# Shifted taps of a causal convolution: added by accumulating transfers on GpSimd's queue in place of VectorE additions

## The chip, the cores and the metric

The kernel runs on one core of a Trainium2 chip. The metric is the device time of one execution in microseconds (us). Five engines have instruction streams of their own and run them in order: TensorE (PE in the profile; PEld is its weight load), VectorE (DVE), ScalarE (ACT), GpSimd (POOL) and SyncE (SP). Transfers are issued by an engine's queue (here SP's and POOL's, a few by ACT) and carried out by 16 DMA engines. Tiles lie in SBUF, 128 partitions wide; products land in PSUM banks.

## The reference: what is computed

One decoder layer on 256 tokens of width 2048, in float32: a combined input projection, two token mixers, an output projection, a gated MLP with a causal depthwise convolution, and a last gate. The change touches the MLP alone:

```python
h = rms_norm(x, ffn_norm_g[i])
u = h @ w_up[i]                                   # 2048 x 11264
a, g = jnp.split(u, 2, axis=-1)                   # 5632 channels each
a = causal_dwconv(a, conv_w[i], conv_b[i])        # width 3, along the tokens
x = x + (jax.nn.gelu(a, approximate=False) * g) @ w_down[i]
```

Per channel the convolution at token s is `w2*a[s] + w1*a[s-1] + w0*a[s-2] + b`, with zeros ahead of the first token.

## The kernel before, in words

**Products.** Each float32 operand is split in two parts, hi (a rounded copy, a CAST on ACT, L1224) and lo (the difference, a subtraction on DVE, L1226), and each product is made of three matmuls: hi x hi, hi x lo, lo x hi (L356, L357, L358 in the MLP). So each block of weights goes through four stations: a load by SP's queue (L1201), the cast on ACT, the subtraction on DVE, the matmuls on PE. Blocks are called units; a plain unit ("p") is one 128-row slice of the weights with 12 matmuls of 512 columns, and some pairs of slices are computed by a seven-product scheme in four short units of 3 to 6 matmuls ("a", "b").

**Groups.** w_up is worked through in 11 groups of 512 + 512 columns (`up_group`, strings in ORDERS give the order of the units of each group: 18 units where the group has one seven-product pair, 20 where it has two). What a group leaves in PSUM goes to EZ (`up_rows`, L1082, and `summed`, L1089), is turned so that channels lie on partitions (`turned`: a 32x32 transpose on DVE, L194, from EZ to Y, and then 16 transfers of 64 KB from Y back to EZ, seen as Z, L200: six from POOL's queue, ten from SP's), and then convolved (`up_act`). All this is done during the units of the next group, between the casts and subtractions of its weights.

**The convolution of one group** has ten jobs: four `scaled(j)` on ACT (each one L1108, which writes w2*a + b to the tile c_, a part of xs, and two L1111, which write w1*a and w0*a to the two taps in Y); `shifted(1)` and `shifted(2)`, which add the taps to c_, one and two tokens later (L1115); `gelu` (ACT, L1118, in place on c_); `gated` (DVE, L1121, times the gate half); `parts_of` (the split in hi and lo for w_down, L150 and L151); and `left` (sums for the seven-product scheme, L456 to L460, one transfer of 512 KB to DRAM, L1068).

**What sets the order.** Each job is hung behind a unit of the next group: ACT_AT holds, for the ten jobs, the number of the unit in the next group. A scheduler in the build lays the instructions out on each engine and may put a job somewhat before or behind that place; the engines then run their lists in order. Parts have a limited number of tiles (eight, four units' worth, while w_up is worked on), so a cast that comes too early waits until PE has released a tile. The last group's jobs don't use ACT_AT: they hang behind fixed units of the work with w_down.

## Time and profile before

| what | value |
|---|---|
| time, median of 3 runs (range) | 1232.63 us (1232.27 to 1233.55) |
| span of the profiled execution, first to last instruction | 1230.1 us |
| PE busy | 1224.3 us (100%) |
| DVE busy | 982.2 us (80%) |
| ACT busy | 749.1 us (61%) |
| POOL busy | 186.8 us (15%) |
| DMA engines, mean busy share over 440 to 930 us | 0.75 |

The profiled execution is told by its span, 1230.1 us from first to last instruction; the median of the runs is 2.5 us above it. The MLP's first half, where the convolutions are, runs from about 440 to 930 us of the span. In the tables below, times of a timeline are from the span's start; "idle before" is how long the engine stood still before an instruction, with what ended that wait; "to landing" is the time from the issue of a transfer to the semaphore that tells of its end. Groups are counted from 1 here: the second group's convolution lies at about 535 to 555 us, the fifth's at 665 to 683, the sixth's at 705 to 724.

### The profile page before, as it was taken

How to read it: one execution, taken by the hardware profiler on the slowest of the kernel's cores; microseconds unless marked ns; L12 is line 12 of the kernel's file. 1: busy time of each engine (PE TensorE's matmuls, PEld its weight loads, DVE VectorE, ACT ScalarE, POOL GpSimd, SP SyncE). 2: the span in 40 equal slices, each digit the busy share in tenths (PEclk: the TensorE clock that was granted, in tenths of full speed). 3: DMA queues.
4: the chain of work that ended last, by engine and by line, in shares of the span. 5: the costliest groups of instructions: out<-in, count | busy, mean ns of one | idle time of the engine just before them, and what ended most of it. 6: DMA issues, size and time to landing. Idle time of an engine off the chain costs nothing.

```text
span 1230.1 us, 16375 instructions
## 1 busy us (share of the span) xinstructions
PE 1224.3 (100%) x5593; PEld 1031.5 (84%) x5593; DVE 982.2 (80%) x1216; ACT 749.1 (61%) x1097; POOL 186.8 (15%) x347
## 2 busy tenths in 40 slices
PE   9999999999999999999999999999999999999998
PEld 7999988888888888888888888888888888888887
DVE  6788857665565689789998898898788999999773
ACT  7567545565554555766676676757657655556652
POOL 2011237243304301011101101110110000050000
PEclk9999999999999999999999999999999999999999
DMA  9566587686557786777687678756797895886670
GB/s 306 182 195 196 171 231 225 186 221 186 163 181 221 221 312 207 242 220 234 210 273 240 182 259 264 226 177 222 228 316 243 296 374 203 266 251 211 200 225 35
DMA packets 131444, 276.89 MB, mean 225 GB/s; under 512 B 14921, under 2 KB 24641, under 8 KB 131233
## 3 DMA queue, kind: packets, MB, share of 16 engines
q1 hardware_dynamic: 119456, 257.40, 66.0%
q0 software_dynamic: 11520, 18.29, 5.3%
q8 instruction: 44, 0.72, 0.2%
q14 instruction: 39, 0.32, 0.1%
q10 hardware_dynamic: 385, 0.16, 0.0%
HBM read 247.99 MB, written 8.93 MB: 209 GB/s over the span
## 4 chain that ended last, share of the span: by engine, by line
PE 99%; DMA 0%; SPq 0%; DVE 0%; ACT 0%; issue 0%; DVEq 0%
PE up L357 12%; PE up L358 11%; PE up L356 11%; PE tg L345 9%; PE tg L346 9%; PE tg L347 9%; PE pg L356 3%; PE pg L357 3%; PE pg L358 3%; PE dnP L1276 1%; PE dnP L1274 1%; PE dnP L1275 1%; PE upP L356 1%; PE upP L358 1%; PE upP L357 1%; PE gt L357 1%
## 5 line engine op out<-in xcount | busy, mean ns | idle before, releaser
L291 DVE TENSOR_TENSOR lo<-raw,hi 128x1024 fp32r<-128x1024 f32 (+3 forms) x130 | 153.3, 1181 | 107.8 <-ACT hi L289 107.4
L358 PE MATMUL up<-part,x2T 128*128 128x512 f32 x608 | 236.6, 389 | 0.0
L357 PE MATMUL up<-part,x2T 128*128 128x512 f32 x608 | 236.5, 389 | 0.0
L1224 ACT CAST part<-raw 128x1024 fp32r<-128x1024 f32 (+1 forms) x144 | 145.5, 1021 | 114.6 <-PE up L358 35.0
L289 ACT CAST hi<-raw 128x1024 fp32r<-128x1024 f32 (+3 forms) x130 | 132.3, 1017 | 123.7 <-PE tg L347 63.4
L1226 DVE TENSOR_TENSOR part<-raw,part 128x1024 fp32r<-128x1024 f32 (+1 forms) x140 | 164.4, 1182 | 26.7 <-ACT part L1224 20.8
L356 PE MATMUL up<-part,x2T 128*128 128x512 f32 x608 | 185.0, 389 | 0.0
L356 PEld LDWEIGHTS up<-part,x2T 128*128 128x128 f32 x608 | 114.2, 188 | 23.6
L358 PEld LDWEIGHTS up<-part,x2T 128*128 128x128 f32 x608 | 114.2, 188 | 23.6
L357 PEld LDWEIGHTS up<-part,x2T 128*128 128x128 f32 x608 | 114.1, 188 | 23.6
L347 PE MATMUL tg<-hi,hT 128*128 128x512 f32 x288 | 113.6, 395 | 0.0
L346 PE MATMUL tg<-lo,hT 128*128 128x512 f32 x288 | 113.2, 393 | 0.0
L345 PE MATMUL tg<-hi,hT 128*128 128x512 f32 x288 | 112.5, 397 | 0.0
L200 POOL DMA_DIRECT2D EZ<-Y x66 | 35.0, 538 | 372.8 <-issue 205.2
L1224 ACT CAST part<-u36r 128x1024 fp32r<-128x1024 f32 (+1 forms) x46 | 47.8, 1041 | 34.6 <-PE up L358 16.3
L1226 DVE TENSOR_TENSOR part<-u36r,part 128x1024 fp32r<-128x1024 f32 (+1 forms) x46 | 55.6, 1209 | 11.0 <-ACT part L1224 6.7
L347 PEld LDWEIGHTS tg<-hi,hT 128*128 128x128 f32 x288 | 54.1, 188 | 11.1
L346 PEld LDWEIGHTS tg<-lo,hT 128*128 128x128 f32 x288 | 54.1, 188 | 10.9
L345 PEld LDWEIGHTS tg<-hi,hT 128*128 128x128 f32 x288 | 53.8, 188 | 10.7
L1226 DVE TENSOR_TENSOR part<-u32r,part 128x1024 fp32r<-128x1024 f32 (+1 forms) x44 | 50.4, 1148 | 11.9 <-ACT part L1224 9.2
L1224 ACT CAST part<-u32r 128x1024 fp32r<-128x1024 f32 (+1 forms) x44 | 43.3, 990 | 21.3 <-PE up L358 9.0
L357 PE MATMUL pg<-lo,hT 128*128 128x430 f32 (+1 forms) x156 | 55.7, 357 | 0.0
(889 smaller groups left out, 2722.0 us busy)
## 6 DMA issues: line engine op xcount, KB each, us to landing
raw<-in_w_up_dram SPq DMA_DIRECT2D x78, 512.0 KB, 5.1
raw<-in_w_in_dram SPq DMA_DIRECT2D x71, 512.0 KB, 4.3
u36r<-in_w_up_dram SPq DMA_DIRECT2D x43, 512.0 KB, 5.0
raw<-in_w_down_dram SPq DMA_DIRECT2D x41, 512.0 KB, 6.2
u32r<-in_w_up_dram SPq DMA_DIRECT2D x34, 512.0 KB, 5.1
raw<-in_w_out_dram SPq DMA_DIRECT2D x32, 512.0 KB, 4.8
xs<-in_w_up_dram SPq DMA_DIRECT2D x21, 512.0 KB, 5.1
w2b<-in_w_down_dram SPq DMA_DIRECT2D x20, 512.0 KB, 5.5
```

Source lines behind the costliest of these rows:

```text
L200: (other if other and (4 * a + b) % 3 else pool).dma_start(out=c[32 * b : 32 * b + 32, a::4], in_=y[32 * a : 32 * a + 32, :, b])
L289: act.copy(hi, raw)
L291: dve.tensor_sub(lo, raw, f32(hi))
L345: pe.matmul(o, ah, hi[:, i, :], start=first, stop=False)
L346: pe.matmul(o, ah, lo[:, i, :], start=False, stop=False)
L347: pe.matmul(o, al, hi[:, i, :], start=False, stop=last)
L356: pe.matmul(o, ah, hi, start=start, stop=False)
L357: pe.matmul(o, ah, lo, start=False, stop=False)
L358: pe.matmul(o, al, hi, start=False, stop=stop)
L1224: act.copy(r32(hi), raw)
L1226: dve.tensor_sub(r32(lo), raw, hi)
L1274: pe.matmul(o, ah, hi, start=first, stop=False)
```

## The change

The two additions L1115 leave DVE. Each becomes one transfer from the tap in Y to c_ with the operation "add", issued by POOL's queue: it reads the tap, adds it to what c_ holds, and writes c_. Both write the same tile, so the second waits for the landing of the first, and `gelu` waits for both. In the same step ACT_AT puts the four scalings behind units 6 to 9 of the next group (9 to 12 before) and the two additions behind units 9 and 11 (13 and 14 before); `gelu`, `gated`, `parts_of` and `left` keep 15 to 18.

```diff
-ACT_AT = (9, 10, 11, 12, 13, 14, 15, 16, 17, 18)
+ACT_AT = (6, 7, 8, 9, 9, 11, 15, 16, 17, 18)
...
             def shifted(d):
-                return lambda: dve.tensor_add(c_[:, :, d:S], taps[d - 1][:, :, 0 : S - d], c_[:, :, d:S])
+                return lambda: pool.dma_start(out=c_[:, :, d:S], in_=taps[d - 1][:, :, 0 : S - d], accum_op=ALU.add)
```

**On ACT, second group.** The list of ACT around this group's last scaling and its gelu (`part_0_...` is the hi part of a unit, named by its number; L1693 empties a PSUM bank). Before:

```order
L1108 ACTIVATE xs<-EZ,cT 128x256
L1111 ACTIVATE Y<-EZ,cT 128x256 x2
L1693 COPY xs<-upP_4878 128x512
L1224 CAST part_0_5041<-u36r 128x1024
L1224 CAST part_0_5062<-u32r 128x1024
L1224 CAST part_0_5093<-u36r 128x1024
L1118 ACTIVATE xs<-xs 128x1024
L1224 CAST part_0_5073<-raw_0_4919 128x1024
```

With the change:

```order
L1108 ACTIVATE xs<-EZ,cT 128x256
L1111 ACTIVATE Y<-EZ,cT 128x256 x2
L1224 CAST part_0_5002<-raw_0_4876 128x1024
L1224 CAST part_0_5030<-raw_0_4904 128x1024
L1224 CAST part_0_5012<-xs 128x1024
L1693 COPY xs<-upP_4878 128x512
L1224 CAST part_0_5062<-u32r 128x1024
L1224 CAST part_0_5042<-u36r 128x1024
L1118 ACTIVATE xs<-xs 128x1024
L1224 CAST part_0_5093<-u36r 128x1024
L1224 CAST part_0_5073<-raw_0_4919 128x1024
```

The last scaling has moved ahead of three casts, the gelu ahead of one; it now waits for the landing of both transfers, and the cast of part 5093 stands behind it.

**On ACT, second group, its first scalings.** Before:

```order
L1224 CAST part_0_4933<-u36r 128x1024
L1224 CAST part_0_4976<-u36r 128x1024
L1108 ACTIVATE xs<-EZ,cT 128x256
L1111 ACTIVATE Y<-EZ,cT 128x256 x2
L1224 CAST part_0_4961<-u32r 128x1024
L1108 ACTIVATE xs<-EZ,cT 128x256
L1111 ACTIVATE Y<-EZ,cT 128x256 x2
L1224 CAST part_0_4946<-xs 128x512
```

With the change:

```order
L1224 CAST part_0_4936<-u36r 128x1024
L1108 ACTIVATE xs<-EZ,cT 128x256
L1111 ACTIVATE Y<-EZ,cT 128x256 x2
L1108 ACTIVATE xs<-EZ,cT 128x256
L1111 ACTIVATE Y<-EZ,cT 128x256 x2
L1224 CAST part_0_4986<-u36r 128x1024
L1224 CAST part_0_4970<-u32r 128x1024
L1108 ACTIVATE xs<-EZ,cT 128x256
L1111 ACTIVATE Y<-EZ,cT 128x256 x2
L1224 CAST part_0_4952<-xs 128x512
```

Parts 4976, 4961 and 4946 are 4986, 4970 and 4952 here. Two scalings now stand ahead of the cast that was first, and a third ahead of the cast of 512 columns from xs.

**On POOL, second group.** Before, the six transfers of one group are followed by those of the next:

```order
L200 DMA EZ<-Y 32x2x256 [waits DMASW1_49]
L200 DMA EZ<-Y 32x2x256 [waits DMASW2_49]
L200 DMA EZ<-Y 32x2x256 [waits DMASW3_49,DVE_49,Activation_49]
L200 DMA EZ<-Y 32x2x256 [waits DMASW4_49]
L200 DMA EZ<-Y 32x2x256 [waits DMASW5_49]
```

With the change the two additions stand between them:

```order
L200 DMA EZ<-Y 32x2x256 [waits DMASW1_49]
L200 DMA EZ<-Y 32x2x256 [waits DMASW2_49]
L1115 DMA xs<-Y 128x4x255 [waits DMASW4_49,Activation_49]
L1115 DMA xs<-Y 128x4x254 [waits DMASW3_49,Activation_49]
L200 DMA EZ<-Y 32x2x256 [waits DMASW5_49,DVE_49,Activation_49]
L200 DMA EZ<-Y 32x2x256 [waits DMASW6_49]
```

The first addition waits for ACT's scalings, the second for the landing of the first, and behind them the next group's transfers stand in the queue.

## The prediction

> **What bounds the kernel now.** I read the page first, then PE's waits, then the table of busy times over the stretch in which the convolutions run.

> ```profile
> span 1230.1 us, 16375 instructions
> PE 1224.3 (100%) x5593; PEld 1031.5 (84%) x5593; DVE 982.2 (80%) x1216; ACT 749.1 (61%) x1097; POOL 186.8 (15%) x347
> PE 99%; DMA 0%; SPq 0%; DVE 0%; ACT 0%; issue 0%; DVEq 0%
> PE warm L100 <- DVE ones L96: 1.1, 1, 1.1
> ...
> 440.00:930.00 490.00, 490.00 (x2163) 405.87 (x2162) 426.40 (x448) 321.56 (x428) 40.10 (x75) 1.00 0.75 237
> ```

> The columns of the last row are the stretch, its sum, and the busy time of PE, PEld, DVE, ACT and POOL, then PE's granted clock, the DMA share and GB/s. PE is busy for all of the 490 us, at full clock, one matmul behind the other; its longest wait anywhere is the 1.1 us at the start, and 99% of the chain that ended last is PE. DVE is busy for 426 of those 490 us, ACT for 322. So nothing that DVE gives up can shorten this stretch: 1230.1 - 1224.3 = 5.8 us is all the idle time PE has, and it lies outside it. The change can only cost time, and costs some where a unit's hi or lo part comes later than PE is ready for it.

> **What is removed, and what hides it.**

> ```profile
> L1115 DVE TENSOR_TENSOR xs<-Y,xs x22: 1209/1213/1217, 506.4 to 946.6; 128x1020 f32<-128x1020 f32 x11, 128x1016 f32<-128x1016 f32 x11
> ```

> 22 x 1.213 = 26.7 us of DVE, all beside busy PE: worth 0.

> **What one accumulating transfer costs (L, from issue to landing).** No such transfer is in the trace. The nearest rows:

> ```profile
> q0 software_dynamic: 11520, 18.29, 5.3%
> ...
> sums<-Sp POOLq DMA_DIRECT2D x9, 512.0 KB, 3.9
> ...
> EZ<-Y POOLq DMA_DIRECT2D x66, 64.0 KB, 2.5
> ...
> EZ<-Y SPq DMA_DIRECT2D x110, 64.0 KB, 2.6
> ...
> DMA to landing us min/median/max: 2.9/3.9/5.2
> ...
> DMA to landing us min/median/max: 3.8/5.1/9.6
> ```

> (The last two are the ranges of the sums' 512 KB to DRAM and of the 512 KB loads on SP's queue in this stretch.) POOL's queue moved 18.29 MB in 5.3% of 1230.1 us, 3.56 us per MB. One addition is 128 x 1020 x 4 B = 0.522 MB, so as a plain copy 1.86 us; what is left of the two POOL rows, 3.9 - 1.9 = 2.0 and 2.5 - 0.2 = 2.3, is the fixed part, about 2.2. An accumulation reads two streams where a copy reads one. If that costs nothing, L = 2.2 + 1.9 = 4.1 (low end 2.9, the fastest row of sums); if the engines' time doubles, 2.2 + 3.7 = 5.9; if it triples (read, read, write, in pieces of 1020 B), 7.8. Weight loads share the engines, and between the fastest and the median load lie 1.3 us of queueing; so 9.1 at the high end. I take doubling with half of that queueing: **L = 6.5** (an estimate). The second addition waits for the first, and the gelu for the second; with about 0.1 us for each of three hand-overs the chain from the end of the last scaling to the gelu is 2L + 0.3 = 13.3 us, where DVE needed two passes of 1.2 us.

> [...]

> **The room in the second group.** Its rows on ACT, SP and PE:

> ```profile
> 526.11 6.52 SPq L200 DMA_DIRECT2D EZ<-Y  x10
> ...
> 535.25 0.60 ACT L1108 ACTIVATE xs<-EZ,cT 128x256 f32<-128x256 f32 x1
> 535.75 0.90 ACT L1111 ACTIVATE Y<-EZ,cT 128x256 f32<-128x256 f32 x2
> 536.55 1.03 ACT L1224 CAST part<-u32r 128x1024 fp32r<-128x1024 f32 x1
> 537.49 0.60 ACT L1108 ACTIVATE xs<-EZ,cT 128x256 f32<-128x256 f32 x1
> ...
> 538.79 0.61 ACT L1224 CAST part<-xs 128x512 fp32r<-128x512 f32 x1
> 539.30 1.06 ACT L1224 CAST part<-raw 128x1024 fp32r<-128x1024 f32 x1
> ...
> 544.86 0.89 ACT L1111 ACTIVATE Y<-EZ,cT 128x256 f32<-128x256 f32 x2
> ...
> 550.21 1.05 ACT L1224 CAST part<-u36r 128x1024 fp32r<-128x1024 f32 x1 [2.08 <-issue]
> 551.17 1.05 ACT L1118 ACTIVATE xs<-xs 128x1024 f32<-128x1024 f32 x1
> ...
> 720.21 1.05 ACT L1224 CAST part<-u36r 128x1024 fp32r<-128x1024 f32 x1 [2.07 <-issue]
> 721.17 1.05 ACT L1118 ACTIVATE xs<-xs 128x1024 f32<-128x1024 f32 x1
> ...
> 540.22 0.39 PE L356 MATMUL upP<-part,x2T 128*128 128x512 f32 x1
> ...
> 552.91 0.62 PE L356 MATMUL up<-part,x2T 128*128 128x512 f32 x2
> ```

> One scaling takes 1.30 us of ACT (535.25 to 536.55), a cast 0.94 (536.55 to 537.49), the half cast 0.51. SP issues the last of its ten transfers at about 532.0, and these land after a median of 2.6 (EZ<-Y on SPq, above); so the first scaling cannot start before 534.6, however early it stands in the list. From there by the new order: two scalings to 537.2, two casts to 539.1, the third scaling to 540.4, the half cast to 540.9, the fourth scaling to 542.2; before, it ended at 545.7.
> - The half cast starts at 540.4 instead of 538.8, 1.6 later. Counted through the order, PE's first product with its tile is the row at 540.22, 0.8 behind that cast's end of 539.4. So **PE loses 0.8** whatever L is.
> - The cast of part 5093 (550.21) now stands behind the gelu. The first product on it is the second of the two at 552.91, at 553.14; so the cast must start by 552.1 and the gelu by 551.1. The room is 551.1 - 542.2 = 8.9, with PE 0.8 late 9.7. **13.3 - 9.7 = 3.6** lost.

> Behind the waiting gelu in ACT's list stand all casts of the coming units, and behind each cast DVE's subtraction and PE. The sixth group has the same order (its gelu at 721.17 stands behind the same cast with the same 2 us gap); I take it alike: 2 x 4.4 = 8.8 us.

> **The other groups.** The fifth stands for the six (first, third, fifth, seventh, ninth and tenth) whose jobs run beside longer units:

> ```profile
> 662.63 1.05 ACT L1224 CAST part<-u36r 128x1024 fp32r<-128x1024 f32 x1
> ...
> 673.12 0.90 ACT L1111 ACTIVATE Y<-EZ,cT 128x256 f32<-128x256 f32 x2
> ...
> 680.27 1.05 ACT L1224 CAST part<-raw 128x1024 fp32r<-128x1024 f32 x1 [1.66 <-PE up L358]
> 681.23 1.05 ACT L1118 ACTIVATE xs<-xs 128x1024 f32<-128x1024 f32 x1
> ...
> 619.87 0.60 ACT L1108 ACTIVATE xs<-EZ,cT 128x256 f32<-128x256 f32 x1
> ...
> 628.02 0.56 ACT L1693 COPY xs<-upP 128x512 f32<-128x512 f32 x1
> ...
> 634.31 1.05 ACT L1118 ACTIVATE xs<-xs 128x1024 f32<-128x1024 f32 x1
> ```

> Its first scaling moves to 662.6; four scalings and two casts end at 669.8 instead of 673.9. Room 681.2 - 669.8 = 11.4, so the gelu is 13.3 - 11.4 = 1.9 late. But here ACT had waited for PE to release a tile (680.27): the casts are three units of 12 matmuls ahead, 3 x 12 x 0.227 = 8.2 us, less 2.3 for the cast and the subtraction: 5.9 of cover, of which I count on 4, since ACT has the next group's PSUM to empty right behind. Lost: 0. (0.227 is the distance of two matmuls, 540.22 and the next; 2163 in 490 us.) In the fourth and eighth the new list has all four scalings in a row: from 619.9 to 625.1, instead of to 628.0; room 634.3 - 625.1 = 9.2; 4.1 late, the cover is somewhere between 0 and 5.9, I take 3: 1.1 each, 2.2 together. The last group's jobs keep their far places: 0.

> **POOL, SP and the DMA engines.**

> ```profile
> 482.35 3.19 POOL L200 DMA_DIRECT2D EZ<-Y  x6 [48.94 <-ACT part L1224]
> 526.66 3.16 POOL L200 DMA_DIRECT2D EZ<-Y  x6 [41.12 <-issue]
> ...
>   ACT part L1224: 12.7, 8
> ```

> On POOL only the next group's six transfers stand behind the additions, due a group of some 44 us after their own predecessors and so over 20 us after the additions: 0, and with that cover gone the scalings behind them would come late in turn. SP is not moved past anything. 22 additions at 3.7 us of all 16 engines add 82 us to a share of 0.75 over 490 us, which makes 0.92; ACT waits for the stretch's weight loads for 12.7 us in 8 waits today (last row), all covered, and I add 1 us for later loads.

> Sum: 8.8 + 2.2 + 1 = **12 us slower**; 1230.1 + 12 in the span, 1232.6 + 12 = **1245 us** by the median.

> **Rivals.**
> - *Copy price.* Where an addition costs no more than a copy, L = 4.1 and the chain 8.5, within every room. What is left is the early scalings, 2 x 0.8 = 1.6: 1234 us, no change that can be measured. For it: POOL's 512 KB row of 3.9. Against it: the second stream read, the pieces of 1020 B, and that the room of 9.7 is used up at L = 4.7.
> - *Triple price*, slower yet. L = 7.8 to 9.1, chain 15.9 to 18.5: second and sixth 2 x 6.2 to 2 x 8.8, fourth and eighth 2 x 3.7 to 2 x 6.3, the six others 0.5 to 3.1 each, with the 1.6 in all 24 to 50 us: 1257 to 1283.
> [...]
> - *Faster.* Only where freed DVE makes a late lo part earlier; but PE waits for none in 490 us. 1229 at best.

> ```profile
> L200 POOL DMA_DIRECT2D EZ<-Y x66: 533/536/567, 482.3 to 915.2; - x66
> ```

> **How the numbers follow.** The forecast (L from 4.9 to 7.6; 1235 to 1255) 0.45; copy price 0.25; triple price 0.22; descriptors held up 0.05; faster 0.03. A measurement here tells 0.2%, 2.5 us, from no change; the copy price is inside that, and three cases are beyond. So faster 0.03, same 0.25, slower 0.72. The range for 8 in 10 goes from the copy price's lower edge, 1232, to 1280, most of the way to the triple price's upper end.

> **What would show it.** L1115 on POOL with its time to landing (5 to 7.5 us if I am right); ACT's gelu waiting for that DMA in every group, longest in the second and sixth; PE's first waits in the stretch, for casts right behind gelu in those two groups and for the half cast ahead of it; DVE 27 us less busy. A landing of about 4 us, or a PE that is still busy 490 of 490 us, proves me wrong in one direction; PE waiting after every gelu, in the other.

## The result, and the profile after

The changed kernel takes **1320.8 us** (median of 4 runs, 1318.4 to 1321.4) where the kernel before took 1232.8 beside it: ratio 1.071, 95% interval 1.0695 to 1.0725. The prediction said 1245, in a range that ended at 1280: slower was right, the size was wrong by a factor of seven.

Rows of the page of the changed kernel (its parts 1 to 3; the last row's columns are packets, MB and the share of the 16 engines):

```profile
span 1318.9 us, 16400 instructions
...
PE 1257.5 (95%) x5593; PEld 1042.2 (79%) x5593; DVE 956.0 (72%) x1194; ACT 745.8 (57%) x1097; POOL 216.3 (16%) x369
...
PEclk9999999999999999989989999989889899999999
...
q0 software_dynamic: 23136, 29.75, 10.5%
```

DVE is 26 us less busy, as forecast, and it is worth nothing. PE, which had 5.8 us of idle time in all, now has 1318.9 - 1257.5 = 61.4: **55.6 us more of waiting**. And the same 5593 matmuls keep it busy for 1257.5 us instead of 1224.3: **33.2 us more**. Its mean granted clock fell from 0.999 to 0.979, in eleven stretches at half clock between 521 and 1045 us (one more lies behind PE's last matmul); PE works for 44 us of them, so **22** of the 33 us are the clock. The other 11 are in the distances of matmuls that the busy time does not count as waits. Waiting and slower matmuls together are the 88.8 us by which the span grew.

The additions on POOL (duration of an issue in ns, then issue to landing), and the waits they set off (sum, times, longest, in us; L1274 and L1275 are products of the down projection):

```profile
L1115 POOL DMA_DIRECT2D xs<-Y x22: 1274/1283/1346, 497.2 to 1023.9; - x22
...
DMA to landing us min/median/max: 6.4/9.6/13.5
```

```profile
ACT xs L1118 <- DMA xs<-Y: 98.3, 10, 14.5
...
PE up L356 <- ACT part L1224: 31.5, 13, 5.0
...
PE up L357 <- DVE part L1226: 9.2, 12, 1.4
...
PE dnP L1274 <- ACT part L1224: 6.1, 1, 6.1
...
PE dn(0, 0)_7985 L1274 <- ACT part L1224: 4.8, 1, 4.8
```

One addition lands after 9.6 us, not 6.5. The gelu waits for it in the second to the eleventh group, 9.8 us each in the mean (the first group's wait is counted elsewhere), and PE then waits for the casts that stand behind the gelu on ACT. (The wait for "dnP" is the last group's, that for "dn(0, 0)" the tenth's: PE is then already at the first products of the down projection.) The second group on ACT, POOL and PE:

```profile
548.48 0.89 ACT L1111 ACTIVATE Y<-EZ,cT 128x256 f32<-128x256 f32 x2
...
565.20 1.06 ACT L1118 ACTIVATE xs<-xs 128x1024 f32<-128x1024 f32 x1 [8.53 <-DMA xs<-Y]
566.17 1.03 ACT L1224 CAST part<-u36r 128x1024 fp32r<-128x1024 f32 x1
...
549.27 1.31 POOL L1115 DMA_DIRECT2D xs<-Y  x1 [11.90 <-ACT Y L1111]
556.22 1.28 POOL L1115 DMA_DIRECT2D xs<-Y  x1 [5.64 <-ACT part L1224]
...
562.40 0.39 PE L358 MATMUL up<-part,x2T 128*128 128x512 f32 x1
567.25 0.80 PE L356 MATMUL up<-part,x2T 128*128 128x512 f32 x1 [4.46 <-ACT part L1224]
...
570.49 0.63 PE L358 MATMUL up<-part,x2T 128*128 128x512 f32 x1
570.92 0.63 PE L357 MATMUL up<-part,x2T 128*128 128x512 f32 x1
```

Two transfers in series, 549.3 to 565.2, then the gelu, then the cast, then PE after 4.5 us of waiting. And what nobody had asked about: after the wait the matmuls stand 0.43 us apart (570.49 and the next) where it had been 0.227. The busy times around it show it as a clock (columns: stretch, sum, busy time of PE, PEld, DVE, ACT, POOL, then PE's granted clock, DMA share, GB/s):

```profile
560.00:566.00 6.00, 2.79 (x13) 1.98 (x11) 0.00 (x0) 0.80 (x1) 0.00 (x0) 1.00 0.90 229
566.00:573.00 7.00, 5.60 (x12) 4.09 (x13) 5.78 (x7) 5.28 (x7) 0.00 (x0) 0.52 0.42 126
573.00:580.00 7.00, 7.00 (x32) 5.74 (x31) 7.00 (x9) 3.06 (x5) 0.00 (x0) 1.00 0.65 184
```

In the 7 us from 566 on, of which the first 1.25 still belong to the wait, PE runs at 0.52 of its clock: 12 matmuls in 5.6 us of work, where 25 would fit at 0.227. A late gelu is paid twice.

### The profile page after: what moved, and what is told of

Same layout as the page of the kernel before. It is cut to its first block, busy times and chain, and to the rows that moved or that the text cites. A ratio compares the mean times of both kernels' runs of the same rounds, so it can differ in the third digit from the quotient of the medians.

```text
span 1318.9 us, 16400 instructions
## 1 busy us (share of the span) xinstructions
PE 1257.5 (95%) x5593; PEld 1042.2 (79%) x5593; DVE 956.0 (72%) x1194; ACT 745.8 (57%) x1097; POOL 216.3 (16%) x369
## 3 DMA queue, kind: packets, MB, share of 16 engines
q0 software_dynamic: 23136, 29.75, 10.5%
## 5 line engine op out<-in xcount | busy, mean ns | idle before, releaser
L357 PE MATMUL up<-part,x2T 128*128 128x512 f32 x608 | 246.0, 405 | 9.4 <-DVE part L1226 9.2
L358 PE MATMUL up<-part,x2T 128*128 128x512 f32 x608 | 242.6, 399 | 0.0
L356 PE MATMUL up<-part,x2T 128*128 128x512 f32 x608 | 198.3, 405 | 32.0 <-ACT part L1224 31.5
L1224 ACT CAST part<-raw 128x1024 fp32r<-128x1024 f32 (+1 forms) x144 | 144.7, 1020 | 99.8 <-PE up L358 20.4
L356 PEld LDWEIGHTS up<-part,x2T 128*128 128x128 f32 x608 | 117.3, 194 | 64.0 <-ACT part L1224 38.4
L357 PEld LDWEIGHTS up<-part,x2T 128*128 128x128 f32 x608 | 117.9, 194 | 43.2 <-DVE part L1226 18.7
L358 PEld LDWEIGHTS up<-part,x2T 128*128 128x128 f32 x608 | 118.1, 194 | 24.3
L200 POOL DMA_DIRECT2D EZ<-Y x66 | 36.0, 552 | 300.6 <-issue 128.3
L1118 ACT ACTIVATE xs<-xs 128x1024 f32<-128x1024 f32 x11 | 11.6, 1057 | 98.3 <-DMA xs<-Y 98.3
L1115 POOL DMA_DIRECT2D xs<-Y x22 | 28.3, 1285 | 214.3 <-ACT Y L1111 118.5
L347 PEld LDWEIGHTS tg<-hi,hT 128*128 128x128 f32 x288 | 54.1, 188 | 11.1
L345 PEld LDWEIGHTS tg<-hi,hT 128*128 128x128 f32 x288 | 53.8, 188 | 10.6
L1224 ACT CAST part<-u36r 128x1024 fp32r<-128x1024 f32 (+1 forms) x46 | 47.6, 1038 | 17.9 <-PE up L358 6.4
## 6 DMA issues: line engine op xcount, KB each, us to landing
raw<-in_w_up_dram SPq DMA_DIRECT2D x78, 512.0 KB, 5.7
raw<-in_w_in_dram SPq DMA_DIRECT2D x71, 512.0 KB, 4.2
u36r<-in_w_up_dram SPq DMA_DIRECT2D x43, 512.0 KB, 5.9
raw<-in_w_down_dram SPq DMA_DIRECT2D x41, 512.0 KB, 6.3
u32r<-in_w_up_dram SPq DMA_DIRECT2D x34, 512.0 KB, 6.8
raw<-in_w_out_dram SPq DMA_DIRECT2D x32, 512.0 KB, 4.8
xs<-in_w_up_dram SPq DMA_DIRECT2D x21, 512.0 KB, 5.9
w2b<-in_w_down_dram SPq DMA_DIRECT2D x20, 512.0 KB, 5.3
```

The lines of the kernel that those rows point to most:

```text
L345: pe.matmul(o, ah, hi[:, i, :], start=first, stop=False)
L347: pe.matmul(o, al, hi[:, i, :], start=False, stop=last)
L356: pe.matmul(o, ah, hi, start=start, stop=False)
L357: pe.matmul(o, ah, lo, start=False, stop=False)
L358: pe.matmul(o, al, hi, start=False, stop=stop)
L1224: act.copy(r32(hi), raw)
```

## The experiments

Times are medians, with the ratio to the kernel before run beside them and its 95% interval; where no interval stands, it is a single run. Rows of waits give the sum, the times and the longest; rows of POOL's issues their number and ns; rows of busy times have the columns named above.

### The list alone, and the transfers alone

```diff
 # early_list: the kernel before with
-ACT_AT = (9, 10, 11, 12, 13, 14, 15, 16, 17, 18)
+ACT_AT = (6, 7, 8, 9, 9, 11, 15, 16, 17, 18)
```

> The kernel before with the new job list (scalings 6, 7, 8, 9) and DVE's two additions kept. Theory (the 88 us are the landing time of two accumulating transfers in series, about 9.6 us each, and what the late gelu sets off): the list alone costs 2 x 0.8 us, 1232 to 1236 us, PE busy 490 of 490 us from 440 to 930 and its clock at 1.00. Rival (the early scalings, which wait on ACT for the transposed rows, are the cause; in the changed kernel they waited 26.4 us in 10 waits): PE waits for casts in most groups, 1250 us or more.

Measured: 1233.2 us, ratio 1.0002 [0.9993, 1.0012].

```profile
440.00:930.00 490.00, 489.92 (x2161) 405.13 (x2161) 425.42 (x448) 319.21 (x427) 40.13 (x75) 1.00 0.75 237
```

The busy times of the stretch: PE loses nothing. The early scalings do wait for their rows, but ACT is far enough ahead for it: the rival falls, and so does the 1.6 us that the prediction charged for it.

```diff
 # acc_old_list: the changed kernel with the old list
-ACT_AT = (6, 7, 8, 9, 9, 11, 15, 16, 17, 18)
+ACT_AT = (9, 10, 11, 12, 13, 14, 15, 16, 17, 18)
```

> The two accumulating transfers with the old job list (scalings 9 to 12, additions 13 and 14, gelu 15). Theory: the last scaling ends later, so the room before the gelu is smaller (about 5.4 us in the second and sixth group, 6.3 in the fourth and eighth, 7.3 in the others) against a chain of 2 x 9.6 + 0.3 = 19.5 us: PE waits of 14.1 x 2 + 10.2 x 2 + 8.2 x 6 = 98 us instead of about 56, and the slower clock after them again about six tenths of that: 1360 to 1400 us. Rival (early scalings are the cause): 1320 us or less. PE's clock in the stretch lower than the 0.96 of the changed kernel.

Measured: 1321.3 us, 1.0706 [1.0685, 1.0728], the same as the changed kernel. The theory's 1360 to 1400 was wrong: the early places of the list bring nothing. (The rival's "1320 or less" is close, but early_list has shown that the early scalings cost nothing.) In the trace of early_list the second group's last scaling ends at 542.8, in that of the kernel before at 545.8, and in most later groups the gain is 0.3 to 3 us, since the rows arrive no earlier; and the transfers landed after 8.7 us here, 0.9 less each. From the last scaling's end to the gelu it is 18.8 us in the mean of ten groups, against 19.5 in the changed kernel. That the two gains cancel is argued from this, not shown.

### The traffic

```diff
 # traffic: the kernel before, and in the first seven groups
     dve.tensor_add(c_[:, :, d:S], taps[d - 1][:, :, 0 : S - d], c_[:, :, d:S])
+    pool.dma_start(out=extra[:, :, d:S], in_=spare_in[:, :, 0 : S - d], accum_op=ALU.add)
 # traffic_in_place: the same, with ahead of the first transfer of a group
+    pool.tensor_copy(uC[:, 4, 1:2], c_[:, 0, 1:2])
```

> The kernel before; beside DVE's two additions the same accumulating transfer (128 x 1020 and 128 x 1016 elements) is issued from POOL in the first seven groups, from columns of x2 into a place that nobody reads: 14 of the 22 transfers, with nobody waiting for them. Theory: no time, 1232 to 1236 us, PE busy 490 of 490; their landing about 9.6 us as in the changed kernel. Rival (the traffic delays weight loads or DVE): 14/22 of the 88 us, up to 1288 us, with weight loads that land later than 5.1 us and PE waits. If the landing here is well below 9.6 us, the landing time is not a price of the transfer but of what surrounds it in the changed kernel.

Measured: 1261.1 us, 1.0222 [1.0198, 1.0247]: neither of the two. The 14 transfers needed nothing of their groups, so POOL issued them one behind the other between 436 and 556 us, each waiting for the one before, and the transposed rows of a group stood behind them. Its waits:

```profile
ACT xs L1111 <- DMA EZ<-Y: 28.7, 3, 23.4
...
PE up L356 <- ACT part L1231: 24.9, 2, 21.7
```

One hole of 21.7 us and one of 3.2; the rest is matmuls at half clock behind them. It shows what a full POOL queue does to the rows behind it; it says nothing on traffic. So again, each pair held to its place:

> As the run traffic, but each pair of transfers is now held to its group's place: POOL first copies one column of the sum that DVE's first addition wrote, into the place to which the transfer adds. 14 transfers in the first seven groups, nobody waits for them. Theory (the 28 us of the run traffic came from the 14 transfers standing one behind the other on POOL ahead of the transposed rows, not from traffic): 1232 to 1238 us, PE busy at least 488 of 490 us, landing 8.5 to 10 us. Rival (the traffic itself delays weight loads or DVE): 1250 to 1265 us.

Measured: 1232.1 us, 0.9994 [0.9984, 1.0003]. The busy times of the stretch, and the landing of the added transfers:

```profile
440.00:930.00 490.00, 490.00 (x2164) 405.73 (x2163) 426.91 (x448) 321.71 (x428) 66.29 (x96) 1.00 0.84 252
```

```profile
DMA to landing us min/median/max: 6.2/8.4/10.1
```

The DMA share rises from 0.75 to 0.84, PE stays busy for 490 of 490 us. The traffic of these 14 costs nothing, and 8.4 us to landing is the price of the transfer where nobody waits for it and nothing else has moved.

### What makes the landing long

```diff
 # prices: beside DVE's additions, into a place that nobody reads, by group
+    pool.dma_start(out=e[:, 4 * d : 1024], in_=i[:, 0 : 1024 - 4 * d], accum_op=ALU.add)
+    pool.dma_start(out=extra[:, 0, d:S], in_=spare_in[:, 0, 0 : S - d], accum_op=ALU.add)
+    pool.dma_start(out=extra[:, :, d:S], in_=spare_in[:, :, 0 : S - d])
+    pool.dma_start(out=extra[0:64, :, d:S], in_=spare_in[0:64, :, 0 : S - d], accum_op=ALU.add)
```

> The kernel before with DVE's additions; beside them, two transfers a group from columns of x2 into a place that nobody reads, of other forms: first and fourth group accumulating in one piece of 4 KB a partition (128 x 1020 and 128 x 1016 elements), second and fifth accumulating a quarter of the bytes (pieces of 1020 B, 128 x 255), third and sixth a plain copy of the full form, seventh accumulating in half of the partitions. Theories of what makes 9.6 us of a landing: (a) the addition itself (two streams read): the copy lands after 4 to 5 us, the 4 KB pieces after 8 to 10, the quarter after 3.5 to 4.5; (b) the pieces of 1020 B, 512 of them: the 4 KB pieces land after 4 to 6, the copy after 8 to 10, the quarter after 3.5 to 4.5; (c) a fixed part of the accumulating kind: the quarter lands after 7 or more. POOL's issue of 1.28 us follows the number of pieces under (b): 0.4 to 0.6 for the quarter and for the 4 KB pieces. Time 1232 to 1240 us.

The rows of three forms (4 KB pieces, a quarter of the bytes, plain copy; four transfers of each):

```profile
L1122 POOL DMA_DIRECT2D uC<-x2T x4: 857/881/947, 435.6 to 480.7; - x4
...
DMA to landing us min/median/max: 6.7/9.0/9.5
...
L1124 POOL DMA_DIRECT2D uC<-x2T x4: 841/848/958, 454.5 to 497.3; - x4
...
DMA to landing us min/median/max: 4.2/5.2/7.2
...
L1126 POOL DMA_DIRECT2D uC<-x2T x4: 777/782/802, 464.4 to 511.9; - x4
...
DMA to landing us min/median/max: 3.3/5.2/6.8
```

Theory (a), the addition: a copy of the same form lands after 5.2 us, the accumulating one after 8.4 to 9.6. The pieces are not it: in 4 KB pieces it is 9.0 all the same, though POOL's issue falls from 1.28 to 0.88 us. A quarter of the bytes saves 3.8 us, so it lands after 5.2, later than the 3.5 to 4.5 that (a) wanted: drawn as a line through 5.2 and 9.0, the accumulating kind has a fixed part of about 3.9 us and 5.1 for all its bytes (an estimate); half of the partitions (two transfers) landed after 6.2, near that line. The run took 1238.7 us. The next kernel takes the addition out where somebody waits for it:

```diff
 # copies: the changed kernel with
-    return lambda: pool.dma_start(out=c_[:, :, d:S], in_=taps[d - 1][:, :, 0 : S - d], accum_op=ALU.add)
+    return lambda: pool.dma_start(out=c_[:, :, d:S], in_=taps[d - 1][:, :, 0 : S - d])
```

> The changed kernel with plain copies in place of the accumulating transfers (the additions are left out: the tap takes the place of the sum). Theory (a), the addition makes the landing long: a copy lands after 4 to 5 us, the chain from the last scaling to the gelu is 8.3 to 10.3 us, within the rooms: 1232 to 1240 us. Theory (b), the 1020 B pieces make it long: landing 8 to 10 us and about the changed kernel's time, 1300 to 1325 us.

Measured: 1256.2 us, 1.0189 [1.0172, 1.0206]. Its transfers:

```profile
L1115 POOL DMA_DIRECT2D xs<-Y x22: 748/753/782, 499.1 to 965.7; - x22
...
DMA to landing us min/median/max: 5.2/6.2/8.9
```

Nearly three quarters of the loss are gone with the addition, so (a) holds; but a copy in this place takes 6.2 us, which is nearly the L that I had predicted for the *addition*, and its cost is 24 us where my own sum for L = 6.5 gave 12. Measured from the last scaling's end to the gelu the chain is 13.4 us in the mean of ten groups (forecast for L = 6.5: 13.3). The clock is 0.999 here: PE has no wait longer than 2.0 us.

### One landing instead of two, shorter landings, a later gelu

```diff
 # acc_first_only: ACT_AT = (6, 7, 8, 9, 9, 14, 15, 16, 17, 18), and
+    if d == 2:
+        return lambda: dve.tensor_add(c_[:, :, d:S], taps[d - 1][:, :, 0 : S - d], c_[:, :, d:S])
     return lambda: pool.dma_start(out=c_[:, :, d:S], in_=taps[d - 1][:, :, 0 : S - d], accum_op=ALU.add)
```

> The new list for the scalings, but only the first addition is an accumulating transfer; the second is DVE's again, put three jobs later (14). Theory: one landing of about 9.6 us fits between the last scaling and the gelu's old place (chain 9.6 + 1.2 + 0.3 = 11.1 us against rooms of 8.9 to 11.4 with up to 5.9 of cover), so no or short waits: 1233 to 1245 us, PE's clock 0.99 to 1.00. Rival (the transfers' traffic on the DMA engines, or DVE held up beside them, costs by itself): half of the 88 us, 1265 to 1285 us.

Measured: 1239.2 us, 1.0044 [1.0029, 1.0058], landing 9.0 us, clock 0.999. Eleven of the 22 transfers cost 6.6 us, not half of 88: it is the two in series that do it.

```diff
 # by_block: each addition in four, issued behind the block's scalings
+    def add(d, j):
+        pool.dma_start(out=c_[:, j, d:S], in_=taps[d - 1][:, j, 0 : S - d], accum_op=ALU.add)
...
+    add(1, j)
+    if j:
+        add(2, j - 1)
```

> The changed kernel with each addition cut in four transfers, one for each block of 256 columns, issued as soon as that block's scalings are done: eight transfers a group of 128 x 255 or 128 x 254 elements; bytes and list are the changed kernel's. Theory (the chain behind the last scaling decides): a quarter lands after about 5.2 us and takes POOL 0.85 us to issue, so two in series and an issue make a chain of about 11.5 us instead of 19.5: 1240 to 1256 us, no stretch at half clock. Rival (the amount moved or POOL's issues decide): 1290 us or more.

Measured: 1272.7 us, 1.0314 [1.0283, 1.0344]: between the two. Its transfers:

```profile
L1105 POOL DMA_DIRECT2D xs<-Y x88: 836/850/1492, 493.3 to 980.8; - x88
...
DMA to landing us min/median/max: 2.7/6.4/9.0
```

Neither forecast was met, and there are stretches at half clock (mean 0.99), where none was expected. The price was again too low: 6.4 us instead of 5.2 for a quarter, a chain of 14.4 instead of 11.5. But the amount moved is the changed kernel's, with four times its issues, and more than half of the loss is gone. Over the kernels with these places for the scalings the loss follows the chain, in the mean of ten groups: 11.3 us cost 6.6 (acc_first_only), 13.4 cost 24 (copies), 14.4 cost 40 (by_block), 19.5 cost 88 (the changed kernel).

```diff
 # gelu_later: the changed kernel with
-ACT_AT = (6, 7, 8, 9, 9, 11, 15, 16, 17, 18)
+ACT_AT = (6, 7, 8, 9, 9, 11, 16, 16, 17, 18)
```

> The changed kernel with the gelu one job place later (16 instead of 15, with the gating product). Theory (what costs is the casts that stand behind the waiting gelu in ACT's list): one more unit's cast stands ahead of it, worth one unit of PE, 2.7 us, in ten groups, and with the shorter waits fewer stretches at half clock: 1280 to 1300 us, landing unchanged at 9.6 us. Rival (the loss does not hang on the gelu's place): 1315 to 1322 us.

Measured: 1318.8 us, 1.0695 [1.0662, 1.0728]: nothing. Two reasons, seen in the lists and in the trace. The scheduler sorts ACT's list by its own costs, and the gelu moved behind one or two more casts in four groups only. And DVE's gating product, which waits for the gelu, kept its place: DVE waited there for 86.3 us where it was 53.5 in the changed kernel, and the lo parts behind it came no earlier. So the run does not test what it was made for. The row of its waits:

```profile
DVE xs L1121 <- ACT xs L1118: 86.3, 10, 10.7
```

```diff
 # last_on_dve: the changed kernel with
+    if q == KF // 4 - 1:
+        return lambda: dve.tensor_add(c_[:, :, d:S], taps[d - 1][:, :, 0 : S - d], c_[:, :, d:S])
```

> The changed kernel with the last group's two additions on DVE again, the other ten groups unchanged. Theory: PE's waits on the down product's casts (6.1 + 4.8 + 0.5 + 0.5 us) and the stretch at half clock behind them (3.4 to 6.8 us, 1.7 to 3.4 lost) go: 1304 to 1309 us. Rival (PE would have waited there anyway, for weights): 1316 to 1321 us.

Measured: 1316.3 us, 1.067 [1.0648, 1.0691]: 4.5 us less, where 12 to 17 were expected. The rival's range, 1316 to 1321, has it, but not for the rival's reason, since one of the two waits did go. PE's waits:

```profile
PE up L356 <- ACT part L1226: 34.3, 13, 6.7
PE up L357 <- DVE part L1228: 9.1, 13, 1.4
PE dn(0, 0)_7985 L1276 <- ACT part L1226: 4.6, 1, 4.6
PE upP L356 <- ACT part L1226: 3.7, 3, 1.4
```

The wait of "dn(0, 0)" stays: it is the tenth group's, and I had booked it to the last one. Only the 6.6 us of "dnP" (6.1 for the cast, 0.5 for the lo part) went, and the waits for casts were 2.8 us longer (34.3 against 31.5).

### Does the loss run from group to group?

By now two readings could explain why the gelu's place made no difference: that each late gelu costs by itself, or that gelu, gating, EZ, the transposition into Y, the next scalings and the next gelu form a loop that has become longer than PE's 42.6 us a group. I took the loop as the theory.

```diff
 # turn_split (changed kernel) and first_split (acc_first_only): 7 of 16 on SP
-    (other if other and (4 * a + b) % 3 else pool)
+    (other if other and (4 * a + b) in (1, 3, 5, 7, 9, 11, 13) else pool)
 # first_all_sp (acc_first_only) and before_all_sp (kernel before): all on SP
-    (other if other and (4 * a + b) % 3 else pool)
+    (other or pool)
```

> The changed kernel with the 16 transfers of the transposed rows shared 7 on SP's queue and 9 on POOL's instead of 10 and 6 (0.65 us each on SP, 0.54 on POOL: the last is issued after about 4.8 us instead of 6.5). Theory (the convolution of one group and of the next form a loop through EZ, Y and xs: gelu, gating, the next group's rows, their transposition, its scalings, the two transfers, gelu; the loop has become longer than PE's 42.6 us a group): each group becomes shorter by 1.2 to 1.9 us, 12 to 19 us in ten, with the clock up to a third more: 1297 to 1309 us. Rival (the gelu's place in ACT's list decides, as the prediction had it): the chain from the last scaling to the gelu is unchanged, 1316 to 1322 us.

> Only the first addition as an accumulating transfer, and the transposed rows 7 on SP's queue and 9 on POOL's. Theory (loop): the run acc_first_only, 1239 us, has a loop just above 42.6 us; 1.2 to 1.9 us less bring it below: 1231 to 1235 us, PE's waits gone. Rival (place in the list): 1238 to 1241 us.

> Only the first addition as an accumulating transfer, and all 16 transfers of the transposed rows on SP's queue (16 x 0.65 = 10.4 us instead of 6.5). Theory (loop): 3.9 us more in each group, of which nothing is covered: 1239 + 10 x 3.9 = 1270 to 1285 us. Rival (place in the list, ACT's lead of three units covers some 4 us of lateness): 1239 to 1250 us.

> Control: the kernel before, DVE's additions, with all 16 transfers of the transposed rows on SP's queue. Theory (loop): DVE's two additions leave the loop some 4 us and more below PE's 42.6 us, so 3.9 us more cost nothing or little: 1232 to 1240 us. Rival (what first_all_sp loses is SP's queue being held up for weight loads, not the loop): as much as first_all_sp loses, 1262 us or more.

Measured: turn_split 1309.5 us, 1.0628 [1.0612, 1.0644]; first_split 1249.7, 1.0135 [1.0118, 1.0152]; first_all_sp 1256.2, 1.0193 [1.0178, 1.0208]; before_all_sp 1239.7, 1.0064 [1.0043, 1.0085]. The control came out as forecast (at the upper edge), the other three did not (turn_split by 0.5 us, first_all_sp between its two forecasts), and first_split became 10 us slower than acc_first_only where the loop wanted 4 to 8 faster. They decide nothing: sharing the 16 transfers otherwise made the scheduler sort ACT's list anew (in all three the four scalings of most groups stand in a row, in first_split behind two more casts). The order was not kept, so more than one thing changed.

```diff
 # acc_alternate and acc_one: the changed kernel with
+    if q not in (1, 3, 5, 7, 9):        # acc_one: if q != 5
+        return lambda: dve.tensor_add(c_[:, :, d:S], taps[d - 1][:, :, 0 : S - d], c_[:, :, d:S])
```

> The changed kernel with the accumulating transfers in every other group only (second, fourth, sixth, eighth, tenth); DVE's additions in the rest, the last group among them. The run last_on_dve has them in ten groups and stands 84 us above the kernel before. Theory (loop): from gelu to first scaling 24.8 us, scalings 7.6, chain 19.5 or about 7, so two groups take 51.9 + 39.4 = 91.3 us against PE's 85.3: 6 us a pair, 30 us in five, less what ACT's lead covers and with no or few stretches at half clock: 1250 to 1264 us. Rival (each late gelu costs the same, whatever the group before did): half of 84, 1272 to 1278 us.

> The changed kernel with the accumulating transfers in the sixth group alone, DVE's additions in all others. Theory (loop): the group before has left slack, so the group is late once, by 19.5 - 11.3 = 8 us, of which ACT's lead of three units covers some 4 to 6: 2 to 4 us, 1234 to 1237 us. Rival (each late gelu costs the same): a tenth of 84, 8.4 us: 1239 to 1243 us.

Measured: acc_alternate 1266.7 us, 1.0277 [1.026, 1.0294]; acc_one 1240.2 us, 1.0062 [1.0047, 1.0077]. PE's waits in acc_alternate, then those in acc_one, and the busy times around the one late gelu of acc_one:

```profile
PE up L356 <- ACT part L1226: 11.7, 5, 4.6
PE dn(0, 0)_7985 L1276 <- ACT part L1226: 5.6, 1, 5.6
PE up L357 <- DVE part L1228: 1.6, 3, 1.1
```

```profile
PE up L356 <- ACT part L1226: 3.5, 1, 3.5
...
PE up L356 <- DVE xs L1696: 0.4, 1, 0.4
PE up L357 <- DVE part L1228: 0.2, 1, 0.2
```

```profile
728.00:734.00 6.00, 2.05 (x8) 1.13 (x7) 2.37 (x3) 3.10 (x4) 0.00 (x0) 0.98 0.45 171
734.00:741.00 7.00, 7.00 (x26) 5.62 (x25) 7.00 (x9) 4.14 (x6) 0.00 (x0) 0.77 0.48 141
741.00:748.00 7.00, 7.00 (x31) 5.48 (x30) 7.00 (x9) 4.94 (x6) 2.26 (x5) 1.00 0.43 120
```

| run | late groups (last one apart) | over early_list, per group | PE's waits, per group | mean clock |
|---|---|---|---|---|
| acc_one | 1 | 7.0 us | 4.1 us | 0.999 |
| acc_alternate | 5 | 6.7 us | 3.9 us | 0.989 |
| last_on_dve | 10 | 8.3 us | 5.2 us | 0.982 |

(Third column: the median less the 1233.2 us of early_list, by the number of groups; fourth: the sum of PE's rows behind late casts, in acc_alternate with 0.5 us of "dn(0, 0)" L1277 and in last_on_dve the same, by the same number.) A late gelu costs nearly the same alone and in every other group, and 1.3 to 1.6 us more where ten stand in a row. The loop falls as the main cause: it wanted 2 to 4 us for acc_one, which lost 8 against the kernel before. (acc_alternate lies between the two forecasts, up to 1264 and from 1272, and that a smaller part is handed on from group to group is not excluded.) Most of a late gelu is paid on the spot: its chain of some 19 us is 8 us longer than the 11 us that the order has room for, and PE waits for 4 to 5 of them; the rest is what ACT's lead covers, about 4 us by this difference. The slow clock behind the wait takes some 2 more, half of the time that PE works at half clock: 1.7 us in acc_one, 2.1 in each of five groups of acc_alternate, 1.8 in each of ten of last_on_dve (a stretch at its start left out). About 1 us a group is in neither.

### PE's clock

```diff
 # stalls: the kernel before, with DVE's second addition in five groups followed by
+    for _ in range({1: 6, 3: 8, 5: 10, 7: 14, 9: 20}.get(q, 0)):
+        dve.tensor_add(taps[0], taps[1], taps[0])
```

> The kernel before with idle additions on DVE behind its second addition (6, 8, 10, 14 and 20 of them, 1.2 us each, in the second, fourth, sixth, eighth and tenth group), no transfer added: PE waits for the lo parts behind them. Theory (PE's waits themselves lower its granted clock): waits of about 2, 5, 7, 12 and 19 us, and behind each of them a stretch of 3.4 or 6.8 us at a clock of 0.5, which costs another 1.7 to 3.4 us each: 1275 to 1290 us. Rival (the clock fell because of the accumulating transfers): the clock stays at 1.00 outside the waits, and the time is 1230 plus the waits.

Measured: 1305.8 us, above the forecast. The scheduler spread the idle additions among DVE's other work: PE waits for 46 us more in all, as expected (45), but in many waits of 4.0 us at most, and its busy time grew by 27.6 us. Around 810 us, first PE's row behind the wait, then the busy times:

```profile
810.16 0.50 PE L357 MATMUL up<-part,x2T 128*128 128x512 f32 x1 [2.53 <-DVE part L1231]
```

```profile
800.00:811.00 11.00, 8.47 (x38) 6.71 (x37) 11.00 (x14) 6.93 (x9) 0.00 (x0) 1.00 0.31 95
811.00:818.00 7.00, 7.00 (x25) 5.60 (x24) 6.49 (x8) 3.56 (x4) 3.73 (x7) 0.76 0.85 250
818.00:825.00 7.00, 7.00 (x32) 5.79 (x31) 5.13 (x7) 4.37 (x9) 0.00 (x0) 1.00 0.76 228
```

No accumulating transfer is in this program, and the clock falls behind PE's waits all the same, here behind one of 2.5 us; over the whole run its mean is 0.985. So the low clock goes with PE's waits and not with the transfers: in traffic_in_place, with 14 of them and PE busy for 490 of 490 us, the mean clock is 1.000. The next kernel was to fill such a wait with work:

```diff
 # acc_one_filled: acc_one, with ahead of the first product behind the late cast
+    for _ in range(16):
+        pe.matmul(st["b"][0, 0], zeros, st["lo"], start=False, stop=False)
```

> The run acc_one (accumulating transfers in the sixth group alone, 1240.2 us), with 16 matmuls by a tile of zeros (they add nothing to the bank) in PE's list ahead of the first product that waits for the cast behind the late gelu: 16 x 0.227 = 3.6 us of work in a wait of 4.2 us. Theory (PE's idle time itself lowers its granted clock afterwards): PE's wait there shrinks to some 0.6 us, the clock stays at 1.00 from 728 to 745 us where acc_one had 0.77 in the 7 us from 734, and the 1.7 us lost to the slow clock come back: 1237.5 to 1239 us. Rival (the clock falls because of the transfers, or in any case): the same stretch at half clock and 1240 us; if the matmuls are not in the wait, up to 1244 us.

Measured: 1237.9 us, 1.0046 [1.0034, 1.0058], an interval that overlaps that of acc_one. The 16 matmuls did not fill the wait: the scheduler placed seven ahead of other products, five and four behind the wait's end, PE still waited for 2.9 us, now for another release, and then ran at 0.77 over the same 7 us. PE's wait, and the busy times behind it:

```profile
PE up L356 <- DVE xs L1699: 2.9, 1, 2.9
```

```profile
734.00:741.00 7.00, 7.00 (x25) 5.61 (x25) 7.00 (x10) 3.95 (x7) 0.00 (x0) 0.77 0.52 152
```

The median lies in the range of the theory, but the wait and the slow stretch are still there, so that is no support for it. The run tells nothing on whether filling a wait keeps the clock; that stays open.

## Why the prediction was wrong, point by point

- **The direction, the chain of waits and the worth of DVE's time were right.** DVE's 26 us are worth 0; the gelu waits for the second transfer in every group; behind it stand ACT's casts, and PE waits for those. Where it would hurt most was wrong (below). What was to show it wrong "in the other direction", PE waiting after every gelu, is what the trace has.
- **The term that failed first is L**, 9.6 us where the sum had 6.5. Both parts of it were too small. The plain copy under it is 6.2 us in this place (5.2 beside it), not 4.1: a fixed part of 2.2, fitted to the sums and the 64 KB rows, was carried to another form, whose issue alone takes POOL 0.75 us and, accumulating, 1.28, where the plain row had 0.54. And the addition adds 3.4 us, not 1.9. By the estimate from the run prices the accumulating kind has 3.9 us fixed and 5.1 for the bytes, where the sum had 2.2 and, with the queueing, 4.3. In the engines' time the doubling was right: the queue's time grew from 5.3% of 1230.1 us to 10.5% of 1318.9, 73 us or 3.3 for each transfer (forecast 3.7), and for a copy, by the 7.8% of 1254.7 us that its page has for the queue, 1.5. The landing is more than the engines' time. The upper end of 9.1 that I had kept for the range was below the median.
- **The working with the right L** comes near PE's waits: with 9.6 us the chain is 2 x 9.6 + 0.3 = 19.5 (measured in the mean of ten groups: 19.5), and the prediction's rooms and covers give 2 x (9.8 + 0.8) + 2 x 7.3 + 6 x 4.1 = 60 us against 55.6 - 6.6 = 49 measured in the ten groups. By group the agreement is less good. The working gives 10.6 us for the second and the sixth, 7.3 for the fourth and the eighth, 4.1 for each of the six others; PE waited for 4.6 and 2.4, for 5.6 and 4.9, and for 4.1 to 6.5 (each wait put to the gelu before or at it). So the total owes something to luck: the second and the sixth, which were to lose most, do not, since their transfers land soonest (chains of 15.8 and 15.6 us, the other eight 18.9 to 21.7), and the six that were to lose nothing lose as much as the fourth and the eighth. The rival "triple price", L = 7.8 to 9.1 and up to 1283 us, had the total at its edge; I had given it 0.22. No run shows what the chance "descriptors held up" (0.05) names: POOL issued the 22 additions in 1274 to 1346 ns each, beside a DVE that was busy for 72% of the span.
- **A term was missing: the clock.** 22 us of the 88 are PE at half clock for some microseconds behind a wait. The sum took a wait for its own length only.
- **The early scalings** (1.6 us) cost 0, and the early list gained 0.3 to 3 us of room where I had reckoned 2.9 to 4.1. **The last group** was put at 0 and costs 4.5 us net. **Contention** (1 us) is 0 with 14 of the 22 transfers. On **POOL and SP** nothing was late behind the additions, as forecast (the scalings waited for their rows for 26.4 us in all, and for 28.2 in early_list); the run traffic shows the price with that cover gone, 21.7 us at once.
- **The rival "copy price"** (1234 us) named the wrong quantity: copies themselves cost 24 us, since they land after 6.2 us and not 4.1.
- **What stays open:** with copies a gelu is, by the prediction's rooms, only 2 us late, which the lead of 4 us should have covered, and 24 us are lost nevertheless, twice what the sum gave for such an L. So L and the clock are not all that failed. PE is idle there for 14 us more in all, in many small waits, 3 us of them in the last group; the other 11 are in its busy time at full clock, in matmuls whose starts stand a little farther apart, as in the changed kernel. Why a lead that covers 4 of 8 us doesn't cover 2 of 2 in each group is not settled.

## What to carry to other kernels

A price for a kind of transfer that the trace doesn't contain is the number to doubt: where it stands twice in series in front of an in-order engine, an error of 3 us in it is 6 in each group. Where PE was busy all the time, a wait cost its length, and then a stretch at half clock where PE's waits in one piece of 3.41 us came to 2.06 us or more; none followed where they came to 1.47 or less (the changed kernel, below). So the question is not only how long PE waits but how close together its waits lie. And an experiment that moves a step under a scheduler has to have its lists compared first: three of these runs moved more than they were meant to, and settled nothing.
